# The pooled half of a mixer's input product taken from x times scale, its gate half after the shift is added, and a memory product in rounded parts

## The chip, the cores and the metric

One core of a Trainium2 chip runs the whole program. The metric is the device time of one execution in microseconds, as the median of several runs. Five engines work side by side, each through its own queue in order: TensorE (PE, with PEld for its weight loads), VectorE (DVE), ScalarE (ACT), GpSimd (POOL, unused here but for constants) and SyncE (SP, which issues every DMA).

## The reference, cut to what matters

Two blocks follow each other, all in fp32, for 512 tokens of 2048 channels. The change is in the first block and in one product of the second.

```
shift, scale, gate = split(silu(c) @ w_mod + b_mod, 3)       # w_mod: 2048 x 6144
h = rms_norm(x) * (1 + scale) + shift                        # 512 x 2048
u, g = split(h @ w_in, 2)                                    # w_in: 2048 x 4096 (w_pin)
pooled_i = centred_window_mean(u_i, w_i) - u_i               # 4 groups of 512 channels, w = 2, 4, 8, 16
y = (pooled_i @ w_grp_i) * pool_scale
x = x + gate * ((y * silu(g)) @ w_out)                       # w_pout
...                                                          # second block
mkv = rms_norm(mem) @ w_mem_kv                               # 256 x 2048 by 2048 x 1024 (w_kv)
```

`shift` and `scale` are one value per channel, the same for every token. So what `shift` adds to a column of u is the same for every token, and a mean over tokens less the token itself takes it out again (the mean divides by the number of tokens inside the sequence). The gate half g needs the whole h.

## The kernel before, in words

**Layout.** The activations of the first block lie with channels on the partitions: 16 chunks of 128 channels by 512 tokens. A large product goes in rounded parts: a number is split into a part that the rounded type holds (`whi`, `h_h`) and the exact rest (`wlo`, `h_l`), and three matmuls (hi by hi, hi by lo, lo by hi) make one (`mm3`, L254). `chan_tile` (L282) holds weights still and moves activations, `tok_tile` the other way round. Banks of PSUM are m0 to m3 and s0 to s3.

**The weight stream.** `Stream` (L34) goes through a plan of tiles in the order of their use. A tile of 512 KB is loaded by SP into one of three buffers (`raw`); `_piece` splits it in two halves, each a cast on ACT (L81) and a subtraction on DVE (L82), and the buffer is loaded anew when the second half has been split (L87 to L89). `take` keeps two halves split ahead; there are four buffers for split halves. `whole` hands a tile over unsplit. A tile with a key isn't split but added up on DVE by `gemv` (L423): DVE multiplies 512 columns of w_mod by a value of silu(c) per partition and adds them to an accumulator (L436). A second stream, `mod`, with up to nine buffers, does that for shift and scale.

**Work beside the main work.** Each part of the main work calls `step`, which gives credit to two lanes of generators (`aside` with a rate): lane 1 makes h, lane 0 does all else. `drain` runs a lane to its end at that place of the program. All engines take their instructions in the order in which this program writes them out.

**Order of the work.** First the memory product: 16 tiles of w_kv, taken whole, 64 matmuls in full fp32 (loop at L483, `mm` at L505) of `memt` (memory rows turned to channels, `mem_pair` L356, an ACT product with a gain out of PSUM). Beside it, rows of x are normed and turned (`x_prep` L391), and the first tiles of w_mod are added up. `modulation` (L455) then makes h two chunks at a time: 8 tiles, each with 256 columns of shift and 256 of scale; `col_sums` (L438) adds over partitions with 8 small matmuls per group, in PE's queue behind the last product of DVE; `make_h` (L443) gives x times scale plus shift on ACT, its cast `h_h`, and DVE makes `h_l` (L467). The input product begins beside that: 4 column tiles of u and 3 of g for each two chunks that are ready (L521 to L527); five more column tiles are begun over the first half of the channels (`begin`, L529) and kept in `early`, to be finished later. Then come the rest of g's and u's first groups, and the other groups in turn, u before g (`pool_loop` L623). `pooled` (L571) makes the window means on DVE in lane 0, `grp_tile` (L603) drains that lane and multiplies by w_grp, `y_out` (L609) takes the result times `pool_scale` times silu(g) and splits it into y_h and y_l. The output product (`tok_tile` with y, L671 on) takes tiles of w_mod for the gate in its stream too (`gate_part` L637).

Of the kernel before, what the change touches and what calls it, by code (L numbers as in the profile page):

```python
# [7 lines left out]
F32 = mybir.dt.float32  # L8
# [6 lines left out]
P = 128  # L15
# [10 lines left out]
# rows of the packed table of vectors  # L26
# [3 lines left out]
# column ranges of w_in_2  # L30
# [3 lines left out]
class Stream:  # L34
    """Weights in the order of their use: loaded ahead, split ahead into a rounded part and the exact rest."""
# [24 lines left out]
    def _piece(self):  # L60
        """One half of a tile of weights is split, or one tile of w_mod added up."""
# [59 lines left out]
def _build(es, tc, nc, x, vecs, bgate, fg, sinks, bforget, w_mod, w_pin, w_grp, w_pout, mem, w_in, w_kv,  # L121
# [7 lines left out]
    # ------------------------------------------------------------ plan of the weight stream  # L129
# [5 lines left out]
    # column tiles of the mixer's input product that begin with the first half of the channels, and how many  # L135
    # of them stand before each pair of chunks of the second half
    EARLY = [2048 + 384, 512, 640, 768, 896]
    AFTER = (1, 2, 2, 0)

# [3 lines left out]
    for kp in range(4):  # L143
        ent(w_pin, kp, [(0, 512, 0)])
        ent(w_pin, kp, [(2048, 384, 0)], n=384)
    ne = 0
    for kp in range(4, 8):
        for c0 in EARLY[ne : ne + AFTER[kp - 4]]:
            ent(w_pin, 0, [(c0, 128, 0)], n=128, kc=8)
        ne += AFTER[kp - 4]  # L150
        ent(w_pin, kp, [(0, 512, 0)])
    for kp in range(4, 8):
        ent(w_pin, kp, [(2048, 512, 0)])

    # products that take tiles of w_grp, by whether the product begins whole or half way
    GRP_AT, GRP_LATE = (3, 6), (4, 6)

    def plan_group(w, segs, n=512, grp=None, gate=None, k0=0):
        for kp in range(k0, 8):
# [3 lines left out]
            if grp is not None and kp in (GRP_AT if k0 == 0 else GRP_LATE):  # L163
                ent(w_grp, 0, [(0, 512, 0)], row0=512 * grp + 256 * (kp == 6))

    plan_group(w_pin, [(512, 512, 0)], grp=0, k0=4)
    plan_group(w_pin, [(2560, 512, 0)], grp=1)
    for g in (2, 3):
        plan_group(w_pin, [(512 * g, 512, 0)])
        plan_group(w_pin, [(2048 + 512 * g, 512, 0)], grp=g)  # L170
# [51 lines left out]
    # ------------------------------------------------------------ side work  # L222
# [12 lines left out]
    def step():  # L235
        """One part of the main work is out: some of the work beside it may follow."""
# [22 lines left out]
    def tile_steps(banks, k0, one, first, last, evac):  # L259
        """One tile of weights: half by half, the last tile of a sum bank by bank."""  # L260
# [21 lines left out]
    def chan_tile(banks, k0, ah, al, first, last, evac=None):  # L282
        """One tile of weights held still; the activations of its rows move."""
# [7 lines left out]
    def tok_tile(banks, k0, ah, al, first, last, n=512, evac=None):  # L291
        """One tile of weights moves; the activations of its rows are held still."""
# [7 lines left out]
    def rsqrt(pool, y, ss, inv, n):  # L300
        """y = 1 / sqrt(ss * inv + EPS), with a Newton step after the table's square root."""
# [1001 lines left out]
```

## Time and profile before

| | |
|---|---|
| device time, median of 3 runs | 2304.04 us (2301.97 to 2304.19) |
| span of the profiled execution | 2301.5 us; its own device time isn't listed apart |
| TensorE busy | 2269.5 us, 99% |
| VectorE busy | 1136.3 us, 49% |
| ScalarE busy | 802.8 us, 35% |
| DMA | 275.16 MB, mean 120 GB/s |

The span runs from the first to the last instruction of the core; the device time is a little longer. "Busy" of TensorE counts a matmul from its start to its modelled end, so that overlapping matmuls count once and a full PE says nothing of its clock; the granted clock stands in rows of their own, 1.00 for 2.4 GHz and 0.50 for 1.2 GHz. DVE's and ACT's shares are means over stages that differ.

### The profile page before, as it was taken

The page shows a single profiled execution, that of the slowest core. Times are in us where ns is not written, and L with a number is a line of the kernel's source. Part 1 is how long each engine was busy: PE and PEld are TensorE (multiplying, and loading weights), DVE is VectorE, ACT ScalarE, POOL GpSimd, SP SyncE. Part 2 cuts the span into 40 slices and gives each one's busy share as a digit, 9 for nine tenths or more (in the row PEclk, how much of TensorE's full clock was granted, in tenths as well). Part 3 has the DMA queues.
Part 4 walks back from the last instruction along what each step waited for, and adds up shares of the span by engine and source line. Part 5 has one row for each costly group of instructions (what it writes and reads, how often), then busy time and mean ns, then how long its engine had stood idle before and what let it go on. Part 6 is the DMA issues. An engine that isn't in the chain of part 4 may idle for free.

```text
span 2301.5 us, 27608 instructions
## 1 busy us (share of the span) xinstructions
PE 2269.5 (99%) x10615; PEld 1862.3 (81%) x10615; DVE 1136.3 (49%) x2009; ACT 802.8 (35%) x1545; POOL 0.2 (0%) x4
## 2 busy tenths in 40 slices
PE   8889999999999999999999999999999999999999
PEld 4578888887889988888888888788888888888887
DVE  3776544356665444566644444455225335226333
ACT  4333332333334443434353434442222222223221
POOL 0000000000000000000000000000000000000000
PEclk9989999999999999999999999999999999999999
DMA  8994333336774332222222222233333333333443
GB/s 290 327 312 125 99 97 98 100 111 220 223 223 138 103 83 74 74 65 75 73 73 64 74 61 77 59 98 101 92 101 93 100 98 95 101 92 97 151 136 110
DMA packets 188203, 275.16 MB, mean 120 GB/s; under 512 B 12082, under 2 KB 98600, under 8 KB 187816
## 3 DMA queue, kind: packets, MB, share of 16 engines
q1 hardware_dynamic: 188072, 273.41, 39.2%
q8 instruction: 83, 1.36, 0.2%
q14 instruction: 48, 0.39, 0.1%
HBM read 264.98 MB, written 8.39 MB: 119 GB/s over the span
## 4 chain that ended last, share of the span: by engine, by line
PE 92%; DMA 4%; DVE 2%; ACT 1%; SPq 1%; issue 1%; DVEq 0%; ACTq 0%
PE m L252 60%; PE s L252 29%; DMA raw<-w_mod 2%; PE s L1020 1%; DMA raw<-w_pin 1%; DMA raw<-w_pout 1%; DVE acc L436 1%; PE s L826 1%; DVE wlo L82 0%; DMA nat<-mem 0%; PE s L1059 0%; PE s L406 0%; DMA xg_d<-xg 0%; PE colb L252 0%; PE s L703 0%
## 5 line engine op out<-in xcount | busy, mean ns | idle before, releaser
L82 DVE TENSOR_TENSOR wlo<-raw,whi 128x512 fp32r<-128x512 f32 (+2 forms) x738 | 493.2, 677 | 733.2 <-ACT whi L81 722.2
L81 ACT CAST whi<-raw 128x512 fp32r<-128x512 f32 (+2 forms) x738 | 443.1, 609 | 862.7 <-PE m L252 412.9
L252 PE MATMUL m<-whi,h_h 128*128 128x512 f32 (+2 forms) x960 | 374.4, 390 | 1.3 <-ACT whi L81 1.3
L252 PE MATMUL m<-wlo,h_h 128*128 128x512 f32 (+2 forms) x960 | 361.9, 377 | 0.8 <-DVE wlo L82 0.7
L252 PE MATMUL m<-whi,h_l 128*128 128x512 f32 (+2 forms) x960 | 362.0, 377 | 0.0
L252 PE MATMUL m<-h_h,whi 128*128 128x512 f32 x736 | 290.9, 395 | 4.3 <-ACT whi L81 4.0
L252 PE MATMUL m<-h_l,whi 128*128 128x512 f32 x736 | 288.3, 392 | 0.4 <-DVE h_l L467 0.4
L252 PE MATMUL m<-h_h,wlo 128*128 128x512 f32 x736 | 288.1, 391 | 0.0
L252 PE MATMUL s<-h_h,whi 128*128 128x512 f32 x544 | 214.2, 394 | 0.0
L252 PE MATMUL s<-h_l,whi 128*128 128x512 f32 x544 | 213.4, 392 | 0.0
L252 PE MATMUL s<-h_h,wlo 128*128 128x512 f32 x544 | 213.3, 392 | 0.0
L252 PEld LDWEIGHTS m<-whi,h_l 128*128 128x128 f32 x960 | 180.4, 188 | 31.7
L252 PEld LDWEIGHTS m<-whi,h_h 128*128 128x128 f32 x960 | 180.6, 188 | 30.7 <-ACT whi L81 1.6
L252 PEld LDWEIGHTS m<-wlo,h_h 128*128 128x128 f32 x960 | 180.8, 188 | 27.6 <-DVE wlo L82 1.6
L252 PEld LDWEIGHTS m<-h_h,whi 128*128 128x128 f32 x736 | 139.2, 189 | 33.1 <-ACT whi L81 4.1
L252 PEld LDWEIGHTS m<-h_h,wlo 128*128 128x128 f32 x736 | 138.9, 189 | 29.4 <-DVE wlo L82 0.3
L252 PEld LDWEIGHTS m<-h_l,whi 128*128 128x128 f32 x736 | 139.2, 189 | 29.0 <-DVE h_l L467 1.1
L252 PEld LDWEIGHTS s<-h_h,whi 128*128 128x128 f32 x544 | 103.5, 190 | 21.6
L252 PEld LDWEIGHTS s<-h_l,whi 128*128 128x128 f32 x544 | 103.4, 190 | 21.6
L252 PEld LDWEIGHTS s<-h_h,wlo 128*128 128x128 f32 x544 | 103.2, 190 | 21.7
L252 PE MATMUL m<-whi,y_h 128*128 128x512 f32 x256 | 102.6, 401 | 1.6 <-DVE t L733 1.5
L252 PE MATMUL m<-whi,y_l 128*128 128x512 f32 x256 | 99.9, 390 | 0.0
(233 smaller groups left out, 2846.6 us busy)
## 6 DMA issues: line engine op xcount, KB each, us to landing
raw<-w_in SPq DMA_DIRECT2D x96, 512.0 KB, 3.8
raw<-w_mod SPq DMA_DIRECT2D x128, 256.0 KB, 5.8
raw<-w_pin SPq DMA_DIRECT2D x61, 512.0 KB, 3.7
raw<-w_in SPq DMA_DIRECT2D x96, 256.0 KB, 2.9
raw<-w_mod SPq DMA_DIRECT2D x32, 512.0 KB, 4.1
raw<-w_pout SPq DMA_DIRECT2D x32, 512.0 KB, 4.0
raw<-w_out SPq DMA_DIRECT2D x32, 512.0 KB, 3.7
raw<-w_in SPq DMA_DIRECT2D x32, 384.0 KB, 3.4
```

What stands on the lines that cost most here:

```text
L81: self.nc.scalar.copy(h3, v)
L82: self.nc.vector.tensor_tensor(out=l3, in0=v, in1=h3.bitcast(F32), op=ALU.subtract)
L252: PE.matmul(ps, lhsT=lhsT, rhs=rhs, start=start, stop=stop)
L436: V.scalar_tensor_tensor(out=acc, in0=v[:, e, :], scalar=w, in1=acc, op0=mult, op1=add)
L826: PE.transpose(b[:, i * P : (i + 1) * P], s, idf)
L1020: PE.transpose(b[:, i * P : (i + 1) * P], pt[:, i * P : (i + 1) * P], idf)
```

## The change

Four things change.

- **The memory product** goes through `tile_steps`: w_kv is split like other weights, `mem_pair` makes the rounded memory rows on ACT and their rest on DVE (out of PSUM), and three matmuls stand where one in full fp32 stood.
- **xs in place of h.** `mod` reads scale alone, 32 tiles of 512 columns; four chunks of x times scale are made at a time (`make_xs`). Four column tiles of u's first group and three of its second go over all 16 chunks in one pass; the last tile of the second group follows by itself. `early` goes.
- **The order of the mixer**: u of all four groups first, then g of all four. Pooling and grouped tiles stand beside u's third and fourth group and the first of g (the table `GRP`); the grouped result times `pool_scale` waits in `yr`, and y is made when a bank of g is evacuated (`evac_g`). `pooled` handles two chunks per instruction.
- **The shift**: its half of w_mod enters the weight stream in 32 tiles of 1024 columns, 2 per pair of chunks, summed on DVE into `sacc`. Ahead of the last pair of u's fourth group 16 small matmuls add it up over partitions, and `add_shift` adds it to the 16 chunks and splits them anew, before and beside g's first group.

```diff
-    for kp in range(4):
+    for kp in range(8):
         ent(w_pin, kp, [(0, 512, 0)])
-        ent(w_pin, kp, [(2048, 384, 0)], n=384)
...
+        ent(w_pin, kp, [(512, 384, 0)], n=384)
+    shifts = [(k, c) for k in range(NK) for c in range(2)]
+    def plan_shift(n):
+        for k, c in shifts[:n]:
+            ent(w_mod, 0, [(1024 * c, 1024, 0)], n=1024, kc=1, row0=k * P, key=("s", c, k))
+        del shifts[:n]
+    for r in range(2):
+        ent(w_pin, 0, [(896, 128, 0)], n=128, kc=8, row0=1024 * r)
+        plan_shift(2)
+    GRP = {2: {2: (0, 0), 4: (0, 1), 7: (1, 0)}, 3: {2: (1, 1), 4: (2, 0), 6: (2, 1)}, 4: {3: (3, 0), 6: (3, 1)}}
+    def plan_group(w, segs, n=512, grp={}, gate=None, shift=0):
+        for kp in range(8):
             if gate is not None:
                 ent(w_mod, kp, [(4096 + 512 * gate, 512, 0)], key=("g", gate, kp))
             ent(w, kp, segs, n=n)
+            plan_shift(shift)
+            if kp in grp:
+                ent(w_grp, 0, [(0, 512, 0)], row0=512 * grp[kp][0] + 256 * grp[kp][1])
+    for g in range(2, 8):
+        plan_group(w_pin, [(512 * g, 512, 0)], grp=GRP.get(g, {}), shift=2)
...
-    mod_plan = [("G", w_mod, j2 * 256, 2, 512, [(256 * kp, 256, 0), (2048 + 256 * kp, 256, 256)], ("h", kp, j2))
-                for kp in range(8) for j2 in range(8)]
+    mod_plan = [("G", w_mod, j2 * 256, 2, 512, [(2048 + 512 * q, 512, 0)], ("h", q, j2)) for q in range(4) for j2 in range(8)]
...
-            S.activation(m[:, c, :], b[:, c * MEM : (c + 1) * MEM], AF.Copy, scale=cols[:, R_MG + k : R_MG + k + 1])
+            S.activation(mh[:, c, :], b[:, c * MEM : (c + 1) * MEM], AF.Copy, scale=g)
+            V.scalar_tensor_tensor(out=ml[:, c, :], in0=b[:, c * MEM : (c + 1) * MEM], scalar=g, in1=r32(mh[:, c, :]), op0=mult, op1=sub)
...
+    def make_xs(k):
+        scl = a0.tile([P, 1], F32, tag="scl", name="scl", bufs=4)
+        V.tensor_tensor(out=scl, in0=colb[:, k : k + 1], in1=bsc1[:, k : k + 1], op=add)
+        S.activation(xnT[k], xnT[k], AF.Copy, scale=scl)
+        S.copy(h_h[k], xnT[k])
...
+        for q in range(5):
             for j in range(8):
+                if q < 4:
                     mod._piece()
                     yield
+                k = 4 * q - 4 + j
+                if q and j < 4:
+                    make_xs(k)
                     yield
+                if q and 1 <= j < 5:
+                    V.tensor_tensor(out=h_l[k - 1], in0=xnT[k - 1], in1=r32(h_h[k - 1]), op=sub)
                     made[0] += 1
                     yield
...
+    def mem_one(ps, b, k, wh, wl, start, stop):
+        c = slice(b * P, (b + 1) * P)
+        mm3(ps, memt[k][0][:, c], memt[k][1][:, c], wh, wl, start, stop)
...
-            w = st.whole()
-            for i in range(2):
-                for j in range(2):
-                    mm(mb[c][i], memt[2 * kp + j][:, i * P : (i + 1) * P], w[:, j, :], start=kp + j == 0, stop=kp == 7 and j == 1)
+            tile_steps(mb[c], 2 * kp, mem_one, kp == 0, kp == 7, ev_mem(c))
...
+    for kp in range(8):
+        while made[0] <= 2 * kp + 1:
             advance(1)
         if kp == 0:
+            pace(0.7)
+        chan_tile(ub, 2 * kp, h_h, h_l, kp == 0, kp == 7)
+        chan_tile(u1, 2 * kp, h_h, h_l, kp == 0, kp == 7)
...
+    def evac_g(g):
+        yh = yhp.tile([P, 4, T], F32R, tag=f"yh{g}", name=f"y_h{g}")
+        def ev(b, ps):
+            k = 4 * g + b
+            y_h[k] = yh[:, b, :]
+            sg = a1.tile([P, T], F32, tag="sg", name="sg", bufs=2)
+            S.activation(sg, ps, AF.Silu)
+            V.tensor_tensor(out=sg, in0=yr[k], in1=sg, op=mult)
+            S.copy(y_h[k], sg)
+            y_l[k] = yp.tile([P, T], F32R, tag=f"yl{k}", name=f"y_l{k}")
+            V.tensor_tensor(out=y_l[k], in0=sg, in1=r32(y_h[k]), op=sub)
+        return ev
...
+    def pool_loop(evac, grp={}, before=None):
         banks = [bank(t) for t in M4]
         for kp in range(8):
+            if before is not None:
+                before(kp)
             chan_tile(banks, 2 * kp, h_h, h_l, kp == 0, kp == 7, evac=evac)
+            if kp in grp:
+                i, cp = grp[kp]
+                grp_tile(i, cp, pool[0])
+                if cp:
+                    aside(grp_out(i), 0.5)
+                if (i, cp) not in ((2, 1), (3, 1)):
+                    pool[0] = new_pool(i + cp, 1 - cp)
...
+    def add_shift():
+        for k in range(NK + 1):
+            if k < NK:
+                S.activation(xnT[k], xnT[k], AF.Identity, bias=shf[:, k : k + 1])
+                S.copy(h_h[k], xnT[k])
+            if k:
+                V.tensor_tensor(out=h_l[k - 1], in0=xnT[k - 1], in1=r32(h_h[k - 1]), op=sub)
+                shifted[0] += 1
+            yield
...
+    def begin_shift(kp):
+        if kp < 7:
+            return
+        drain()
+        sb = bank("s3", "shb")
+        for k in range(NK):
+            mm(sb[:, k : k + 1], sacc[k // 8][:, (k % 8) * P : (k % 8 + 1) * P], ones[:, 0:1], start=True, stop=True)
+        V.tensor_tensor(out=shf, in0=sb[:, 0:NK], in1=cols[:, R_BMOD : R_BMOD + NK], op=add)
+        aside(add_shift(), 0.5, 1)
+    pool_loop(evac_u(2), grp=GRP[2])
+    def after_shift(kp):
+        while shifted[0] <= 2 * kp + 1:
+            advance(1)
+    pool_loop(evac_u(3), grp=GRP[3], before=begin_shift)
+    pool[0] = new_pool(3, 0)
+    pool_loop(evac_g(0), grp=GRP[4], before=after_shift)
     for g in range(1, 4):
-        if g > 1:
-            pool_loop(evac_u)
-        pool_loop(evac_g, grp=g)
-        aside(y_out(g), 0.25)
+        pool_loop(evac_g(g))
```

## Rows read from the trace of the kernel before

**Rows 1.** The page: the span, each engine's busy time (share of the span, instructions), and in 40 equal slices of the span the tenths in which TensorE was busy and the clock granted to it.
```profile
span 2301.5 us, 27608 instructions
...
PE 2269.5 (99%) x10615; PEld 1862.3 (81%) x10615; DVE 1136.3 (49%) x2009; ACT 802.8 (35%) x1545; POOL 0.2 (0%) x4
...
PE   8889999999999999999999999999999999999999
...
PEclk9989999999999999999999999999999999999999
```

**Rows 2.** Busy time by stage (the view by stretches): stretch in us, its length, then busy us and instructions of PE, PEld, DVE, ACT and POOL, the mean granted clock, the DMA share and GB/s. The stages are the memory product, the part in which h is made beside the first columns of the mixer's input product, the rest of the mixer, and all that follows.
```profile
13.00:80.00 67.00, 67.00 (x216) 33.86 (x216) 30.82 (x80) 28.94 (x74) 0.00 (x0) 1.00 0.92 310
80.00:202.00 122.00, 107.63 (x473) 88.55 (x472) 100.41 (x174) 41.90 (x70) 0.00 (x0) 0.87 0.89 276
202.00:516.00 314.00, 314.00 (x1387) 260.01 (x1386) 155.57 (x261) 100.71 (x169) 0.00 (x0) 1.00 0.33 100
516.00:2301.50 1785.50, 1777.78 (x8534) 1477.39 (x8532) 848.74 (x1488) 626.94 (x1226) 0.00 (x0) 1.00 0.35 104
```

**Rows 3.** TensorE's instructions in order of time, alike ones merged: start in us, us, engine, line, operation, tiles, count, and in brackets the idle time before and what ended it.
```profile
13.20 9.55 PE L252 MATMUL m<-raw,memt 128*128 128x512 f32 x16
...
59.27 20.77 PE L252 MATMUL m<-raw,memt 128*128 128x512 f32 x48
79.87 1.84 PE L252 MATMUL colb<-ones,acc 128*128 128x1 f32 x16
85.72 0.79 PE L252 MATMUL m<-h_h,whi 128*128 128x512 f32 x1 [4.01 <-ACT whi L81]
...
88.87 0.63 PE L252 MATMUL m<-h_l,whi 128*128 128x512 f32 x1
89.30 0.63 PE L252 MATMUL m<-h_h,wlo 128*128 128x512 f32 x1
```

**Rows 4.** Groups of TensorE's instructions from 0 to 240 us, shapes apart: tiles, shapes, count, busy us, mean ns of one, idle before it.
```profile
L252 PE MATMUL m<-raw,memt 128*128 128x512 f32 x128 | 60.6, 614 | 0.0
...
L252 PE MATMUL colb<-ones,acc 128*128 128x1 f32 x128 | 19.7, 278 | 9.6 <-DVE acc L436 9.5
```

**Rows 5.** What TensorE waited for between 80 and 200 us: tile and line, who was waited for, us in total, times, longest.
```profile
PE colb L252 <- DVE acc L436: 9.5, 7, 3.3
PE m L252 <- ACT whi L81: 4.0, 1, 4.0
```

**Rows 6.** Stretches of 4 us in which the clock fell and came back (columns as in rows 2).
```profile
108.00:112.00 4.00, 3.07 (x18) 2.89 (x19) 4.00 (x8) 0.00 (x0) 0.00 (x0) 0.80 1.08 361
112.00:116.00 4.00, 4.00 (x11) 3.13 (x10) 3.12 (x7) 3.18 (x5) 0.00 (x0) 0.50 1.10 350
116.00:120.00 4.00, 4.00 (x16) 3.20 (x16) 4.00 (x7) 0.51 (x2) 0.00 (x0) 0.84 1.09 354
...
160.00:164.00 4.00, 3.92 (x17) 3.79 (x17) 3.01 (x8) 0.44 (x1) 0.00 (x0) 0.50 0.90 273
164.00:168.00 4.00, 4.00 (x11) 3.03 (x11) 1.05 (x2) 3.47 (x6) 0.00 (x0) 0.50 1.08 334
168.00:172.00 4.00, 4.00 (x18) 3.29 (x17) 4.00 (x7) 0.00 (x0) 0.00 (x0) 0.94 0.90 266
```

**Rows 7.** Groups of ScalarE's instructions from 0 to 530 us (columns as in rows 4).
```profile
L81 ACT CAST whi<-raw 128x512 fp32r<-128x512 f32 x146 | 88.9, 620 | 146.1 <-PE m L252 97.6 <-PE s L252 37.2 <-issue 9.7
...
L450 ACT ACTIVATE xq<-xq,shf,scl 128x512 f32<-128x512 f32 x16 | 13.0, 813 | 45.4 <-DVE scl L448 45.4
...
L451 ACT CAST h_h<-xq 128x512 fp32r<-128x512 f32 x16 | 9.9, 620 | 0.5
L565 ACT ACTIVATE sg<-m 128x512 f32<-128x512 f32 x12 | 7.2, 598 | 9.7 <-PE m L252 9.7
```

**Rows 8.** The same of VectorE, and at the end one line of its instructions in order of time.
```profile
L82 DVE TENSOR_TENSOR wlo<-raw,whi 128x512 fp32r<-128x512 f32 x145 | 99.0, 690 | 147.8 <-ACT whi L81 139.7 <-PE s L252 8.0
L436 DVE SCALAR_TENSOR_TENSOR acc<-raw,csil,acc 128x512 f32<-128x512 f32 x112 | 77.0, 749 | 0.0
...
L592 DVE TENSOR_TENSOR pl<-praw,ph 128x512 fp32r<-128x512 f32 x16 | 11.1, 693 | 11.1 <-ACT ph L591 11.1
L590 DVE SCALAR_TENSOR_TENSOR praw<-tr,up 128x512 f32<-128x512 f32 x16 | 11.1, 693 | 0.6
...
L467 DVE TENSOR_TENSOR h_l<-xq,h_h 128x512 fp32r<-128x512 f32 x16 | 10.9, 691 | 6.7 <-ACT h_h L451 6.7
...
L434 DVE TENSOR_SCALAR acc<-raw,csil 128x512 f32<-128x512 f32 x16 | 7.0, 484 | 0.0
...
L448 DVE TENSOR_TENSOR scl<-colb,bsc 128x2 f32<-128x2 f32 x8 | 1.2, 155 | 0.0
...
59.64 4.06 DVE L436 SCALAR_TENSOR_TENSOR acc<-raw,csil,acc 128x512 f32<-128x512 f32 x6
```

**Rows 9.** DMA issues by line, each with its count, KB and the median us from issue to landing: the two of w_pin and w_grp from 202 to 516 us, that of w_mod from 500 to 560.
```profile
raw<-w_pin SPq DMA_DIRECT2D x46, 512.0 KB, 3.7
raw<-w_grp SPq DMA_DIRECT2D x8, 512.0 KB, 3.7
...
raw<-w_mod SPq DMA_DIRECT2D x9, 512.0 KB, 4.3
```

**Rows 10.** The instructions that read the tile y_h, over the whole span: count, least, median and largest ns, first and last start in us.
```profile
L252 PE MATMUL m<-whi,y_h x256: 387/389/799, 515.8 to 701.0; 128*128 128x512 f32 x128
```

More of the change, by code (lines that the diff above doesn't have):

```diff
@@ L318, in _build @@
     mkv = kvpool.tile([P, 2, 1024], F32, name="mkv")
-    ep = ExitStack()
-    earlyp = ep.enter_context(tc.tile_pool(name="early", bufs=1, side="right"))
-    early = {}
+    yhs = ExitStack()
+    yhp = yhs.enter_context(tc.tile_pool(name="yhp", bufs=1))
+    xq = [yhp.tile([P, 4, T], F32, tag=f"yh{q}", name=f"xq{q}") for q in range(4)]
+    xnT = [xq[k // 4][:, k % 4, :] for k in range(NK)]
     p0 = ExitStack()
@@ L375, in _build @@
     mem_pair(1)
-    xq = [a0.tile([P, 4, T], F32, name=f"xq{q}") for q in range(4)]
-    xnT = [xq[k // 4][:, k % 4, :] for k in range(NK)]
     ssq = a0.tile([P, 6, 4], F32, name="ssq")
@@ new lines, in pooled @@
+        src, s0, span = up, 8 - w // 2, 1
+        while span < w:
+            n = T + w - 2 * span
+            t = a1.tile([P, 2, 528], F32, tag=f"tr{span % 3}", name="tr", bufs=1)
+            V.tensor_tensor(out=t[:, :, :n], in0=src[:, :, s0 : s0 + n], in1=src[:, :, s0 + span : s0 + span + n], op=add)
+            src, s0 = t, 0
+            span *= 2
+            yield
+        hw = w // 2
+        e0 = edg[:, i, 0, :hw].unsqueeze(1).to_broadcast([P, 2, hw])
+        V.tensor_tensor(out=src[:, :, :hw], in0=src[:, :, :hw], in1=e0, op=mult)
@@ new lines, in pooled @@
+        if hw > 1:
+            e1 = edg[:, i, 1, : hw - 1].unsqueeze(1).to_broadcast([P, 2, hw - 1])
+            V.tensor_tensor(out=src[:, :, T - hw + 1 : T], in0=src[:, :, T - hw + 1 : T], in1=e1, op=mult)
+        praw = a1.tile([P, 2, T], F32, tag="praw", name="praw")
+        V.scalar_tensor_tensor(out=praw, in0=src[:, :, :T], scalar=1.0 / w, in1=up[:, :, 8:520], op0=mult, op1=sub)
+        yield
+        S.copy(ph, praw)
+        yield
+        V.tensor_tensor(out=pl, in0=praw, in1=r32(ph), op=sub)
@@ L595, in _build @@
+        yield
     grp_banks = {}
     def new_pool(i, cp):
-        ph = [a1.tile([P, T], F32R, tag=f"ph{c}", name="ph") for c in range(2)]
-        pl = [a1.tile([P, T], F32R, tag=f"pl{c}", name="pl") for c in range(2)]
-        aside(pooled(i, cp, ph, pl), 0.32)
-        return ph, pl
+        ph = a1.tile([P, 2, T], F32R, tag="ph", name="ph")
+        pl = a1.tile([P, 2, T], F32R, tag="pl", name="pl")
+        aside(pooled(i, cp, ph, pl), 0.3)
+        return [ph[:, c, :] for c in range(2)], [pl[:, c, :] for c in range(2)]
@@ L607, in grp_tile @@
         chan_tile(grp_banks[i], 0, pool[0], pool[1], cp == 0, cp == 1)
-    def y_out(i):
-        yrs = {}
-        for ct in range(5):
-            if ct < 4:
-                yrs[ct] = a1.tile([P, T], F32, tag="yr", name="yr", bufs=2)
-                k = 4 * i + ct
-                V.scalar_tensor_tensor(out=yrs[ct], in0=grp_banks[i][ct], scalar=cols[:, R_PS + k : R_PS + k + 1], in1=sg[:, ct, :],
-                                       op0=mult, op1=mult)
-                S.copy(y_h[k], yrs[ct])
-            if 0 < ct < 5:
-                k = 4 * i + ct - 1
-                V.tensor_tensor(out=y_l[k], in0=yrs[ct - 1], in1=r32(y_h[k]), op=sub)
-            yield
@@ L623, in pool_loop, with grp_out, ev @@
-    def pool_loop(evac, grp=None):
+    def grp_out(i):
+        for ct in range(4):
+            k = 4 * i + ct
+            S.activation(yr[k], grp_banks[i][ct], AF.Copy, scale=cols[:, R_PS + k : R_PS + k + 1])
+            yield
+    def evac_g(g):
+        yh = yhp.tile([P, 4, T], F32R, tag=f"yh{g}", name=f"y_h{g}")
+        def ev(b, ps):
+            k = 4 * g + b
[6 more added lines that the diff above has]
+            V.tensor_tensor(out=y_l[k], in0=sg, in1=r32(y_h[k]), op=sub)
+        return ev
@@ new lines, in _build, with shift_part @@
+    sacc = [a1.tile([P, 1024], F32, name=f"sacc{c}") for c in range(2)]
+    def shift_part(c, k, v):
+        w, v = csil[:, k : k + 1], v[:, 0, :]
+        if k == 0:
+            V.tensor_scalar(out=sacc[c], in0=v, scalar1=w, scalar2=None, op0=mult)
+        else:
+            V.scalar_tensor_tensor(out=sacc[c], in0=v, scalar=w, in1=sacc[c], op0=mult, op1=add)
+    more["s"] = shift_part
+    shf = a1.tile([P, NK], F32, name="shf")
+    shifted = [0]
+    def add_shift():
[6 more added lines that the diff above has]
+                shifted[0] += 1
+            yield
@@ L759, in _build @@
     ys.close()
+    yhs.close()
     us = ExitStack()
```

149 lines of the change are left out of this document (27 added, 122 removed).

## The prediction

> **What bounds the kernel now.** I first read the page's totals and slices: PE is busy for 2269.5 of 2301.5 us, and only the first slices show less than full tenths or a clock below full [rows 1]. So only two things can move the time: PE work that goes away, and time near the start in which PE waits or runs at its lower clock. The busy time by stage says where that is [rows 2]. From 13 to 80 us, the memory product, PE has no gap and a full clock. (Its first 16 records, at 0.60 us each, show a slow start, [rows 3].) From 80 to 202, the part in which h is made piece by piece, it is busy 107.6 of 122 us at a mean granted clock of 0.87. From 202 to 516 it is full, and so nearly to the end.
>
> One matmul of rounded parts costs 314.0 / 1387 = 0.226 us of PE time at the full clock [rows 2]; its listed 0.39 us overlaps with the next. At the lower level two starts lie 0.43 apart, at 88.87 and 89.30 [rows 3]. A memory matmul in full fp32 shows as two records, and 48 records take 20.77 us: 0.433 a record, 0.865 a matmul [rows 3]. Sixteen records of column sums take 1.84 us, 0.23 a sum [rows 3].
>
> What is lost between 80 and 202: of 473 records 112 are column sums (the 128 of [rows 4] less the first 16), 112 x 0.115 = 12.9 us; the other 361 x 0.226 = 81.6. That makes 94.5 of 122 us: **27.5 us are lost**. PE waited 9.5 us for the accumulators under the column sums and 4.0 for a split weight [rows 5], and behind such waits the clock fell to 1.2 GHz (0.50 in the rows) for some 6 to 10 us at a time [rows 6]. DVE was busy 100.4 us of it and DMA moved 276 GB/s [rows 2]: 33.5 MB of w_mod had to be read and summed up before h was whole.
>
> **The change, part by part.**
>
> *Memory product.* 64 fp32 matmuls (55.4 us) become 192 of rounded parts (43.5): **11.9 us of PE work go** if the clock stays full. But the parts must be split: 32 casts on ACT at 0.62 (19.8 us, on 28.9 busy: 48.7) [rows 2, 7] and 32 subtractions on DVE at 0.69 (22.1), with 16 subtractions of 256 columns out of PSUM, which before doesn't have; between 0.15 us (a tiny operation's price, [rows 8]) and 0.75 (512 columns with a scalar, [rows 8]) I take 0.4, since half the columns stand nearer the middle: 6.4 us. DVE comes to 30.8 + 22.1 + 6.4 = 59.3 us [rows 2, 8], while PE's work, transposes included, is 67 - 11.9 = 55 us. So DVE, not PE, fills the stage, in order behind norms and transposes, and PE starts some 2 us later since its first weights must be split. I take 63 us from 13 on, DVE at 94%: the end at 76 in place of 80, so **8 us of the 11.9 are given back** (0 to 12; beyond 12 is a rival).
>
> *Column sums.* Eight groups of 8 sums become four of 8 and sixteen single ones later: 64 to 48, **3.7 us go**.
>
> *xs in place of h.* Half of w_mod, 16.8 MB, stands ahead of the pooled half. Seven banks now take all 16 chunks in one pass: 336 matmuls, 76 us, so each quarter of w_mod (4 chunks, two pairs) has 19 us of PE cover. At the pace of 0.7 a step, a quarter's 16 parts take 23 steps, 1.63 pairs: 15.5 us and 1.84 of sums, 17.4. In these DVE does 16 products at 0.68 (6 in 4.06 us, [rows 8]), 4 low parts at 0.69 and the weights' low parts, 1.63 pairs of 2.4 us: 17.5. DMA brings 4.2 MB and 1.5 of weights, 328 GB/s, under the 350 to 361 of the rows in which it ran without a pause [rows 6]. Level, not over, and the last 3.6 pairs have no more of it. **Of the 27.5 us, I leave 2 of waits and one fall of the clock, 3.5** (8 us at half rate, less overlap): 5.5 (0 to 16, a wait and a fall at each of three quarters).
> Ahead of the first product stay the scale's addition, an ACT product with one scalar (0.81, [rows 7]), a cast (0.62) and a subtraction (0.69). The weights are split already, which was the 4.0 us of before. I take **1.9 us of idle and 2.5 of slow clock** (2 to 8).
>
> *Shift beside it.* 32 tiles of 1024 columns enter the weight stream, 2 per pair, on the same three buffers and the same SP queue. DVE takes 32 x 1.36 = 43 us for them, beside 16 pairs' splits (22), six grouped tiles' (8) and the pooling of three groups (some 28, from 0.69 per 512 columns, [rows 8]): 101 of the 120 us of two loops and six grouped tiles. It fits on average. The buffers are tighter: three tiles per pair means each buffer turns once in 24 x 0.226 = 5.4 us. A tile lands in 3.7 us alone and 4.3 beside w_mod [rows 9], and a weight tile then needs two casts and a subtraction, 2.0, and the next issue 0.1: 6.4. A grouped tile, 5.4 us of PE for one buffer, follows every second or third pair and gives the slack back (10 tiles in 21.7 us leave a buffer 6.5). I take **3 us lost** (0 to 13, every one of 14 pairs late by 0.95).
> The Trainium skill, "DMA: Bandwidth & Descriptors", section "Anatomy of one DMA", gives 2.0 us and bytes over 436 GB/s per transfer, fitted for transfers issued from GpSimd. For 512 KB that is an estimate of 3.2 us; the turn would be 5.3 and this term 0. The rows with 3.7 to 4.3 on the queue used here speak against it.
>
> *Pooling.* Two chunks go in one instruction at the same cost per column. The low part now stands three dependent operations of 1024 columns deep. At two grouped tiles (the third group's) the side work has 16 steps for what needs 20 to 28, so it is drained with PE behind it: praw, ph and pl at 1.3 + 1.2 + 1.3, less two halves of lead (2.7 us): **2.5 us** for both (0 to 6).
>
> *Adding the shift.* Its 16 sums wait for the last of four ACT copies out of a bank, with the group's last pair behind them in PE's queue: some **1.2 us**. Then ACT has 16 x 1.24 us beside casts and copies, 29 us for five pairs and a grouped tile (33 us): **1.5 us** (0 to 5).
>
> *Gates last.* Each of four evacuations is Silu, product, cast, subtraction per bank, and the next bank's Silu stands in ACT's queue behind the cast, which waits for DVE: 0.6 + 0.7 + 0.6 and the handovers come to 2 us against 1.36 us of PE per bank, so the fourth bank is freed about 2.5 us after PE's last matmul, and the next loop needs it after 2.0. With a table load: **2.5 us** over all (0 to 5). Before, products waited for nobody here [rows 2].
>
> Nothing after the mixer is touched: the first product of y stands at 515.8 [rows 10], and what follows keeps its length. SP issues 64 transfers of w_mod where it issued 128 (512 KB each, not 256), and one more of w_pin.
>
> **The sum.** 11.9 + 3.7 + 27.5 = 43.1 gone; 8 + 5.5 + 4.4 + 3 + 2.5 + 2.7 + 2.5 = 28.6 back: 14.5 us. The profiled span 2301.5 gives 2287.0. Its own device time isn't listed apart; the median of the runs, 2304.04, stands 2.5 us above the span, and I keep that: **2289.5 us**.
>
> **The rivals.**
> 1. *The memory product runs at the lower clock* (slower). Fed by DVE it waits often, where fp32 never did. At 0.43 a matmul its work is 82.6 us, 39 more, and the 8 us of waits vanish in it: -14.5 + 31 = +16.5, **2320**. It decides once some 110 of the 192 run so: (14.5 + 8) / 0.204. For it: at 85% busy the clock was at half for a quarter of the time [rows 2, 6]. Against: a PE at half rate is slower than DVE, becomes full, and a full PE was given its clock back each time [rows 6]. Chance 0.10. The Trainium skill, "TensorE: Matmul & The Clock Gate", section "HAM oscillation", tells of a kernel throttled anew at every tile because each waited for data; by that rule this rival would come. The trace agrees as far as long waits go and shows none so short.
> 2. *Everything is covered.* Memory ends at 72, quarters cost nothing, the small terms halve: 43.1 - 4 - 3 - 6.5 = 30, **2274**. For it: even between 80 and 202 DVE had 18% to spare [rows 2]. Chance 0.17.
> 3. *Three buffers don't feed 1.6 MB per pair.* The shift term is 13: gain 4.5, **2299.5**. Chance 0.12.
> 4. *The rounded product isn't shorter*, because DVE or the transfers (22 MB by the last w_kv tile) end it at 80 as before: gain 10.5, **2293.5**. Chance 0.13.
> The forecast keeps 0.48, its own range 2282 to 2297.
>
> **How the numbers follow.** What a measurement here can tell from no change is 0.2%, 4.6 us. Faster takes the forecast, rivals 2 and 4 and a third of 3: 0.82. Same is the rest of 3, 0.08; slower is rival 1, 0.10. The range reaches down into rival 2 and up past rival 3, and leaves out rival 1 and the far end of 2: 2271 to 2303.
>
> **What the changed profile would show.** Memory's last matmul near 76; first product of xs near 80; the seven banks done near 169; PE's first product of y near 501 in place of 515.8; granted clock above 0.95 from 80 to 200. A clock of 0.5 over the memory stage, or PE waiting for casts between 180 and 300 at every pair, would show rivals 1 or 3. Wrong it would also be if work after the mixer moved.

## The result, and the profile after

The changed kernel takes **2325.8 us** (median of 4 runs, 2324.93 to 2326.93) beside 2304.1 for the kernel before on the same chip: ratio 1.0093, 95% interval 1.0079 to 1.0108. It is 21.7 us slower where 14.5 us less were forecast: 2325.8 against 2289.5, a miss of 36.3 us.

First the page: PE's busy time hardly changed, but its first slices did (compare [rows 1]).

```profile
span 2323.5 us, 27655 instructions
...
PE 2269.0 (98%) x10647; PEld 1873.0 (81%) x10647; DVE 1154.5 (50%) x1982; ACT 845.8 (36%) x1621; POOL 0.2 (0%) x4
...
PE   6899989999999999999999999999999999999999
...
PEclk9899999999999999999999999999999999999999
```

The stages, cut at the changed kernel's own ends (columns as in [rows 2]): the memory product up to the first column sum; the part that makes xs; the pooled half with the shift beside it; g's first group; the other gates; all that follows.

```profile
13.00:84.50 71.50, 61.00 (x279) 45.45 (x278) 54.12 (x123) 46.50 (x109) 0.00 (x0) 1.00 0.84 287
84.50:165.00 80.50, 68.14 (x282) 55.97 (x282) 55.13 (x104) 31.97 (x54) 0.00 (x0) 0.85 0.53 170
165.00:345.00 180.00, 169.96 (x728) 137.45 (x727) 107.88 (x136) 57.84 (x97) 0.00 (x0) 0.96 0.58 183
345.00:400.00 55.00, 55.00 (x242) 45.16 (x241) 37.31 (x53) 33.84 (x55) 0.00 (x0) 1.00 0.33 96
400.00:534.80 134.80, 132.05 (x579) 108.05 (x578) 49.96 (x75) 45.06 (x77) 0.00 (x0) 1.00 0.33 98
534.80:2323.50 1788.70, 1779.83 (x8535) 1478.61 (x8533) 848.18 (x1487) 626.47 (x1226) 0.00 (x0) 1.00 0.35 104
```

The first product of y (the tile's row, as [rows 10]) and, over the first 600 us, what PE waited for (columns as in [rows 5]):

```profile
L247 PE MATMUL m<-whi,y_h x256: 387/389/799, 534.8 to 723.7; 128*128 128x512 f32 x128
```

```profile
PE colb L247 <- DVE acc L433: 9.2, 5, 4.5
...
PE s L247 <- ACT ph L559: 6.1, 2, 5.1
PE m L247 <- DVE wlo L82: 4.0, 10, 1.2
PE m L247 <- ACT whi L81: 3.5, 3, 2.2
PE m L247 <- ACT sg L593: 3.2, 5, 1.5
PE s L247 <- DVE pl L561: 3.1, 3, 1.9
PE m L247 <- ACT h_h L445: 3.1, 1, 3.1
```

The first product of y stands 19.0 us later than before. What follows takes 1788.7 us instead of 1785.7; that part does the same work in every kernel of this document, and its length in their traces lies between 1785.5 and 1790.6 us, so these 3 us don't stand out as an effect of the change. I price each stage at the full clock as the prediction did, 0.2264 us a matmul and 0.115 a record of the column sums; what a stage takes beyond that is lost. From 84.5 to 165 the 282 records hold 64 of column sums: 218 x 0.2264 + 7.4 = 56.7 of 80.5 us, **23.8 lost**. From 165 to 345, 32 of 728 belong to the shift's sums: 161.3 of 180, **18.7 lost**. From 345 to 400 nothing, from 400 on 134.8 - 579 x 0.2264 = 3.7. The memory product ends at 84.5 instead of 79.9.

The views that follow show how the loss from 84.5 to 165 comes about. PE in order of time (columns as in [rows 3]), lines with a wait, and one at the lower clock:

```profile
89.56 0.80 PE L247 MATMUL m<-h_h,whi 128*128 128x512 f32 x1 [3.06 <-ACT h_h L445]
...
104.94 3.81 PE L247 MATMUL colb<-ones,acc 128*128 128x1 f32 x16 [4.50 <-DVE acc L433]
...
110.04 0.63 PE L247 MATMUL m<-h_h,whi 128*128 128x512 f32 x1
...
128.20 0.38 PE L247 MATMUL colb<-ones,acc 128*128 128x1 f32 x2 [1.37 <-DVE acc L433]
...
150.74 0.38 PE L247 MATMUL colb<-ones,acc 128*128 128x1 f32 x2 [2.79 <-DVE acc L433]
```

What DVE, then ACT, waited for from 88 to 155 us:

```profile
DVE wlo L82 <- ACT whi L81: 13.3, 9, 2.0
DVE scl L443 <- PE colb L247: 5.6, 3, 3.2
```

```profile
ACT xq L444 <- DVE scl L443: 44.5, 11, 10.6
```

And one round of it in order of time, DVE first, then ACT:

```profile
93.95 1.41 DVE L433 SCALAR_TENSOR_TENSOR acc<-raw,csil,acc 128x512 f32<-128x512 f32 x2
95.28 0.15 DVE L443 TENSOR_TENSOR scl<-colb,bsc 128x1 f32<-128x1 f32 x1
97.29 0.56 DVE L82 TENSOR_TENSOR wlo<-raw,whi 128x384 fp32r<-128x384 f32 x1 [1.86 <-ACT whi L81]
```

```profile
95.46 0.72 ACT L444 ACTIVATE xq<-xq,scl 128x512 f32<-128x512 f32 x1 [2.02 <-DVE scl L443]
...
96.74 1.55 ACT L81 CAST whi<-raw 128x384 fp32r<-128x384 f32 x3
```

PE stands still for an accumulator at the second to fourth quarter, and behind the wait of 4.50 us the 16 records of column sums take 3.81 us instead of the 1.84 of [rows 3]. DVE is not full over the stage (55.1 of 80.5 us). In the round shown, ACT waits 2.02 us at an xs for a scale, which stands on DVE behind two products of w_mod; ACT's cast of a weight stands behind that xs, and DVE then waits 1.86 us for the cast. Each engine, in order, waits for the other. Such rounds make up DVE's 13.3 us. Of ACT's 44.5 us, 31.9 are of another kind: four waits in which a whole quarter's column sums are still to come.

### The profile page after: what moved, and what is told of

Read it like the earlier page. It is cut to its first block, busy times and chain, and to the rows that moved or that the text cites. A ratio compares the mean times of both kernels' runs of the same rounds, so it can differ in the third digit from the quotient of the medians.

```text
span 2323.5 us, 27655 instructions
## 1 busy us (share of the span) xinstructions
PE 2269.0 (98%) x10647; PEld 1873.0 (81%) x10647; DVE 1154.5 (50%) x1982; ACT 845.8 (36%) x1621; POOL 0.2 (0%) x4
## 4 chain that ended last, share of the span: by engine, by line
PE 88%; DVE 4%; ACT 3%; DMA 2%; issue 1%; SPq 0%; ACTq 0%; DVEq 0%
PE m L247 57%; PE s L247 29%; PE s L1038 1%; DVE acc L433 1%; DVE wlo L82 1%; DMA raw<-w_pin 1%; ACT whi L81 1%; PE s L844 1%; DMA raw<-w_pout 1%; DMA raw<-w_grp 0%; ACT junk L384 0%; DVE sg L594 0%; PE colb L247 0%; DVE tr L546 0%; PE s L1077 0%
## 5 line engine op out<-in xcount | busy, mean ns | idle before, releaser
L82 DVE TENSOR_TENSOR wlo<-raw,whi 128x512 fp32r<-128x512 f32 (+3 forms) x772 | 513.6, 675 | 759.2 <-ACT whi L81 753.2
L81 ACT CAST whi<-raw 128x512 fp32r<-128x512 f32 (+3 forms) x772 | 460.8, 608 | 925.6 <-PE m L247 423.4
L247 PE MATMUL m<-h_h,whi 128*128 128x512 f32 x768 | 304.9, 397 | 5.8 <-ACT h_h L445 3.1
L247 PE MATMUL m<-h_l,whi 128*128 128x512 f32 x768 | 301.7, 393 | 0.0
L247 PE MATMUL m<-h_h,wlo 128*128 128x512 f32 x768 | 301.5, 393 | 0.0
L247 PE MATMUL s<-h_h,whi 128*128 128x512 f32 x512 | 200.3, 391 | 0.0
L247 PE MATMUL s<-h_l,whi 128*128 128x512 f32 x512 | 200.1, 391 | 0.0
L247 PE MATMUL s<-h_h,wlo 128*128 128x512 f32 x512 | 199.9, 390 | 0.0
L247 PEld LDWEIGHTS s<-h_h,whi 128*128 128x128 f32 x512 | 96.6, 189 | 20.1
L247 PE MATMUL m<-wlo,y_h 128*128 128x512 f32 x256 | 100.4, 392 | 0.3 <-DVE wlo L82 0.3
```

Of the source, the lines that this page charges most:

```text
L81: self.nc.scalar.copy(h3, v)
L82: self.nc.vector.tensor_tensor(out=l3, in0=v, in1=h3.bitcast(F32), op=ALU.subtract)
L247: PE.matmul(ps, lhsT=lhsT, rhs=rhs, start=start, stop=stop)
```

## The experiments

Times are medians, ratios are to the kernel before run beside them (2304.1 to 2304.6 us each time), and "less" or "slower" without a name is against the changed kernel's 2325.8. Line numbers in a kernel's rows are its own.

**The part that makes xs.** Column sums later in PE's queue:

```diff
+            late = 2 if q > 1 else 0
...
+                if q and j == late:
+                    col_sums(q - 1)
+                k = 4 * q - 4 + j - late
...
-            if q < 4:
-                col_sums(q)
```

> The changed kernel with the column sums of the second to fourth quarter put two tiles of w_mod later in TensorE's queue; the same work. Theory A (VectorE is only a few us late at the three sums, since a quarter's last products come bunched, and each wait of 1.4 to 4.5 us also costs a fall of the clock): the waits under the sums between 100 and 155 us go below 1 us each, the granted clock stays near 1 and the time falls by 10 to 16 us (2310 to 2316). Rival B (VectorE has too much work per quarter): the wait moves to the first product that needs the next chunks, and the time falls by 0 to 3 us.

2321.95 us (2321.48 to 2323.88), ratio 1.0078 [1.0063, 1.0093]: 3.9 less, between the two. PE's waits for accumulators fall from 9.2 to 4.8, one of 3.8 stays. Where PE stands in its queue is a small part.

The scales of four chunks added at once, before the next w_mod products; ACT's xs issued ahead of the next w_mod tile; side work at 0.5 a step instead of 0.7:

```diff
+    def make_scl(q):
+        scl4[q] = a0.tile([P, 4], F32, tag="scl", name="scl", bufs=2)
+        V.tensor_tensor(out=scl4[q], in0=colb[:, 4 * q : 4 * q + 4], in1=bsc1[:, 4 * q : 4 * q + 4], op=add)
...
+                if q and j == late:
+                    col_sums(q - 1)
+                    make_scl(q - 1)
+                if q and 0 <= j - late < 4:
+                    make_xs(k)
                 if q < 4:
                     mod._piece()
...
-            pace(0.7)
+            pace(0.5)
```

> The changed kernel with the four scales of a quarter added in one VectorE operation behind the sums, and each chunk's product with its scale issued on ScalarE ahead of VectorE's next w_mod tile, not behind it; the pace is 0.5 in place of 0.7 since there are fewer parts, so that a quarter takes the same stretch of the program. Theory A (VectorE and ScalarE wait for each other: a scale stands behind 1.35 us of w_mod, a cast behind that scale's two operations, a low part behind the cast, 13.3 us of VectorE's waits in 65 us): those waits fall below 6 us, the waits under the sums below 3 us in all, and the time falls by 10 to 15 us (2311 to 2316). Rival B (too much work per quarter): 0 to 3 us.

2313.28 us (2310.55 to 2315.21), 1.0034 [1.0022, 1.0047]: **12.5 less**, theory A. The stage, what DVE waited for in it from 88 to 155 us, and what PE still waited for an accumulator:

```profile
84.50:165.00 80.50, 77.13 (x356) 64.02 (x355) 59.83 (x102) 35.33 (x61) 0.00 (x0) 0.96 0.60 197
```

```profile
DVE scl L444 <- PE colb L247: 6.0, 3, 3.0
DVE wlo L82 <- ACT whi L81: 5.0, 5, 1.4
```

```profile
PE colb L247 <- DVE acc L433: 0.3, 1, 0.3
```

In the same 80.5 us PE issues 356 records instead of 282, at 0.96 of the clock instead of 0.85, and its waits under the sums fall from 9.2 us to 0.3. Priced as above, 292 matmuls and 64 records of sums are 73.5 of 80.5 us: 7.0 lost, where it was 23.8. DVE does more work in the stage, not less, so most of the loss was the order in the queues and not the volume. The edit has three parts, and these runs don't tell how much each gives. (The pace goes with the other two: a quarter now has 12 parts of side work in place of 16, so at 0.5 it takes 24 steps of the main work, and 23 before.)

More split halves ahead (six buffers, four ahead) while u's first group runs:

```diff
+        st.ahead = 4 if kp < 6 else 2
+        if kp == 7:
+            st.hlp = hlp
```

> The changed kernel with six buffers for split weight halves and four split ahead, in place of four and two, while the seven banks of u are summed (the pool of the first stage has room for it). Theory A (VectorE idles there since the next cast waits for a buffer that TensorE still reads, so it cannot work ahead of the sums): VectorE's waits for the cast between 90 and 155 us shrink, and the time falls by 6 to 12 us (2314 to 2320). Rival B (order and volume of the w_mod products decide, not the buffers): within 2 us.

2327.83 us (2325.88 to 2329.66), 1.0102 [1.0087, 1.0117]: no gain. DVE's wait for ACT's casts stays 13.5 us; more buffers for split halves don't mend this order of the queues.

**The shift's stream.** The shift left out (its half of w_mod is neither read nor added, so the gates are computed without it):

```diff
-        for k, c in shifts[:n]:
+        for k, c in []:
...
-        aside(add_shift(), 0.5, 1)
```

> The changed kernel without the shift: its half of w_mod isn't loaded or summed, and nothing is added to the chunks, so the gate half lacks it. Theory A (the shift beside the pooled half costs what is lost from 165 to 345 us, 18.7 us, and its sums 3.7): the time falls by 18 to 22 us (2304 to 2308). Rival B (pooling two chunks at once, drained in front of PE, costs most of it by itself): it falls by 4 to 10 us, and PE still waits for pooled parts at 308 us.

2304.91 us (2302.76 to 2308.02), 0.9998 [0.9989, 1.0007]: 20.9 less, theory A. The shift and all that hangs on it cost that; the prediction's terms for it were 3 in the stream, 2.7 in adding it, and its 16 sums.

A fourth buffer for loaded tiles, from the pooled half until the last group of g begins, so for all of the shift's tiles in it:

```diff
+            self.turn = (self.turn + 1) % 4
+            pl = self.raw2 if self.turn == 0 else self.raw
...
+    st.raw2 = p1.enter_context(tc.tile_pool(name="raw2", bufs=1))
+    st.bufs = 4
```

> The changed kernel with a fourth buffer for loaded tiles while the shift's tiles are in the weight stream. Theory A (three tiles per pair turn three buffers in 4.0 us of landing and 2.0 of splitting, longer than the 5.4 us of a pair, so splits come late and with them pooling): PE's waits between 200 and 330 us (9.2 us) go below 3 us and the time falls by 8 to 14 us against the changed kernel (2312 to 2318). Rival B (the pooling's own order and rate hold PE): 0 to 2 us.

2313.01 us (2310.39 to 2317.43), 1.0032 [1.0019, 1.0046]: **12.8 less**, theory A. How one more buffer does that, the changed kernel shows: ACT from 283 us on, and SP's issues.

```profile
287.17 1.14 ACT L81 CAST whi<-raw 128x512 fp32r<-128x512 f32 x2 [1.75 <-DMA raw<-w_pin]
293.23 0.62 ACT L81 CAST whi<-raw 128x512 fp32r<-128x512 f32 x1 [4.91 <-DMA raw<-w_pin]
...
300.04 1.14 ACT L81 CAST whi<-raw 128x512 fp32r<-128x512 f32 x2 [3.35 <-DMA raw<-w_grp]
```

```profile
283.17 0.38 SPq L51 DMA_DIRECT2D raw<-w_pin  x1
284.37 2.22 SPq L51 DMA_DIRECT2D raw<-w_mod  x2
289.15 0.38 SPq L51 DMA_DIRECT2D raw<-w_pin  x1
```

The next weight tile is issued 6.0 us after the last, when its buffer comes free, and its cast begins 4.1 us later still. From 165 to 345 us ACT's casts wait like this in all:

```profile
ACT whi L81 <- DMA raw<-w_pin: 36.0, 11, 5.6
```

With the fourth buffer this is 17.3 us, and in the kernel without the shift none. The low part behind the cast holds up DVE, and the pooling stands behind it there, in order. DVE's next lines, and PE's at the grouped tile:

```profile
300.69 0.69 DVE L82 TENSOR_TENSOR wlo<-raw,whi 128x512 fp32r<-128x512 f32 x1 [2.05 <-ACT whi L81]
301.30 1.23 DVE L546 TENSOR_TENSOR tr<-up 128x1036 f32<-128x1036 f32 x1
...
305.84 1.23 DVE L557 SCALAR_TENSOR_TENSOR praw<-tr,up 128x1024 f32<-128x1024 f32 x1
```

```profile
308.20 0.80 PE L247 MATMUL s<-ph,whi 128*128 128x512 f32 x1 [5.11 <-ACT ph L559]
...
310.48 0.63 PE L247 MATMUL s<-ph,whi 128*128 128x512 f32 x1
```

So PE never waits for a cast at a pair; it stops at the grouped tiles, where the late pooling is drained, and goes on at the lower clock. With the fourth buffer the stage and PE's waits for pooled parts (6.1 and 3.1 us in the changed kernel) read

```profile
165.00:345.00 180.00, 177.19 (x785) 145.51 (x784) 117.90 (x149) 70.92 (x117) 0.00 (x0) 0.99 0.59 189
```

```profile
PE s L252 <- ACT ph L564: 1.3, 1, 1.3
...
PE s L252 <- DVE pl L566: 0.8, 1, 0.8
```

The other explanation, that pooling is merely credited too slowly:

```diff
-        aside(pooled(i, cp, ph, pl), 0.3)
+        aside(pooled(i, cp, ph, pl), 0.6)
...
-                    aside(grp_out(i), 0.5)
+                    aside(grp_out(i), 1.0)
```

> The changed kernel with the side work of pooling issued at twice its rate (0.6 and 1.0 a step in place of 0.3 and 0.5), so that it is out before its grouped tile. Theory A (TensorE waits for pooled parts that the side work issued too late, 8.8 us in waits at 237, 263 and 308 us, and twice loses its clock): these waits go below 2 us in all and the time falls by 8 to 12 us (2314 to 2318). Rival B (the parts are late because the weight stream with three buffers is late in these loops): the time falls by 0 to 3 us.

2330.49 us (2329.05 to 2332.9), 1.0115 [1.01, 1.013]: 4.7 slower. Pooling issued earlier stands ahead of the low parts on DVE, and PE now waits for splits too (3.9 us from 84 to 345, none in the changed kernel), with 3.9 still waited for ph.

**The memory product.** Back in full fp32 (`mem_pair` makes one fp32 tile again):

```diff
-            tile_steps(mb[c], 2 * kp, mem_one, kp == 0, kp == 7, ev_mem(c))
+            w = st.whole()
+            for i in range(2):
+                for j in range(2):
+                    mm(mb[c][i], memt[2 * kp + j][:, i * P : (i + 1) * P], w[:, j, :], start=kp + j == 0, stop=kp == 7 and j == 1)
```

> The changed kernel with one part undone: the memory product again in 64 full-fp32 matmuls of unsplit weights, the rest as changed. Theory A (the rounded product is fed too slowly by VectorE and ScalarE and ends at 84.5 us where fp32 ended at 80): the product ends near 80, the first product of xs starts near 85 in place of 89.6, and the time falls by 4 to 6 us against the changed kernel (2320 to 2322). Rival B (the stage is set by its transfers, or what is won is waited for again at the next sums): within 2 us of the changed kernel. My recorded forecast, by which the rounded parts win 4 us, would make it 4 us slower than the changed kernel.

2320.87 us (2316.39 to 2323.46), 1.0076 [1.0058, 1.0094]: 4.9 less, theory A. The first column sum comes at 79.2 us, nearly as before (79.9); the first product of xs follows only at 86.7, behind a wait of 5.7 us for a split weight. And the rounded product alone in the kernel before (the edit reversed):

> The kernel before with one part of the change alone: the memory product in rounded parts. Theory A (fed by VectorE and ScalarE it ends some 4.6 us later than fp32): 3 to 6 us slower than the kernel before (2307 to 2310). Rival B (in the kernel before the stage that follows is bound by transfers, which go on meanwhile, so that the delay is made good): within 2 us of it. By my recorded forecast it would be 4 us faster.

2311.72 us (2309.97 to 2314.15), 1.0031 [1.002, 1.0042]: 7.6 slower than before, more than the 3 to 6 expected, first column sum at 84.4, PE waiting 4.5 us for the first h. Two comparisons from either side agree on the sign, not on the size. Why the stage is long: what DVE, then ACT, waited for from 13 to 84.5 us in the changed kernel.

```profile
DVE wlo L82 <- ACT whi L81: 8.5, 6, 2.5
DVE meml L364 <- ACT memh L363: 4.9, 8, 1.1
DVE rx L301 <- ACT rs_t L300: 2.2, 5, 1.2
DVE ssx L393 <- ACT junk L384: 1.8, 3, 0.7
```

```profile
ACT memh L363 <- DVE meml L364: 11.6, 7, 3.0
```

DVE's 54.1 us of work and 17.4 of waits, all for ACT, are the 71.5 us of the stage. The 11.6 us looked like two memory chunks sharing a tile, so each got its own:

```diff
-        mh = a0.tile([P, 2, MEM], F32R, tag="memh", name="memh", bufs=4)
+            mh = a0.tile([P, MEM], F32R, tag=f"memh{c}", name="memh", bufs=4)
```

> The changed kernel with each chunk of the memory rows in a tile of its own, and nothing else. Theory A1: the product ends 3 us or more before 84.5 and the time falls by 3 to 5 us (2321 to 2323). Rival A2 (VectorE's work sets the end): 0 to 2 us.

2324.54 us (2322.12 to 2326.2), 1.0084 [1.007, 1.0098], 1.3 less: my first theory fell. The sums still begin at 84.7 us, and ACT still waits 10.6 us for meml. Then more split halves ahead, over the memory product alone:

```diff
+    hl2 = p0.enter_context(tc.tile_pool(name="hl2", bufs=6))
+    st.hlp, st.ahead = hl2, 4
```

> The changed kernel with six buffers for split halves and four halves split ahead over the memory product alone (two ahead, four buffers, as before, from there on). Why does the rounded product end at 84.5 us instead of 76? Theory L (lookahead): PE waits because a half is asked for two halves after it was begun and a transposed memory chunk stands between; with four ahead TensorE's waits for whi and wlo there (3.5 and 4.0 us) fall below 3, the first column sum moves from 84.5 to 77 to 81 and the time falls by 3 to 8 us: 2318 to 2323. Rival V (volume): VectorE's low parts, norms, transposed chunks and column products fill the stage whatever the order: the column sum stays within 2 us of 84.5 and the time within 2 us of 2325.8.

2319.65 us (2317.58 to 2324.01), 1.0071 [1.0054, 1.0088]: 6.2 less, in the range of theory L, but not by its way. The first column sum:

```profile
85.47 0.38 PE L247 MATMUL colb<-ones,acc 128*128 128x1 f32 x2 [2.01 <-DVE acc L433]
```

PE is done with the product at 83.5, 1.0 us earlier, and then waits for DVE's accumulator: DVE's queue ends the stage. The first product of y comes 3.8 us earlier (531.0). These are won in the next part, where the wait of 4.50 us is down to 0.2 and 301 records in place of 282 stand in the 80.5 us; how the edit does that, no run shows. With the other two repairs in, the same edit gave nothing (below), so I don't count it as a cause of its own.

**Together.** The fourth buffer and the scales at once (the two diffs above; "the run before" in the expectation is the kernel with three repairs, which follows here):

> As the run before, but with the memory product in rounded parts as in the change. Theory A: 2325.8 less 12.5 and 12.8, 2299 to 2302. Rival B: 2305 to 2310. Its difference to the kernel with three repairs prices the rounded product once more: 4 to 6 us if what it loses isn't made good later.

2298.07 us (2296.99 to 2301.07), 0.9971 [0.9959, 0.9983]; a little faster than theory A's 2299 to 2302: the two gains of 12.5 and 12.8 add up (27.7 together). With the memory product in fp32 as well:

> The changed kernel with three repairs at once: the memory product back in fp32, ScalarE's product with the scale ahead of the w_mod tile, and the fourth buffer beside the shift. Theory A (three separate losses, alone worth 4.9, 12.5 and 12.8 us, that add up): 2294 to 2298, some 6 to 10 us faster than the kernel before. Rival B (each repair wins the same time, since what is early in one stage waits in the next): 2305 to 2310.

**2293.88 us** (2292.63 to 2296.08), 0.9952 [0.9939, 0.9964]: faster than both kernels, and 4.2 us faster than with the rounded product, the third price for it beside 4.9 and 7.6. Its stages (columns as above), and its first product of y:

```profile
84.50:165.00 80.50, 78.23 (x350) 64.46 (x351) 56.56 (x96) 34.28 (x60) 0.00 (x0) 0.94 0.59 190
165.00:345.00 180.00, 177.21 (x779) 143.88 (x779) 126.49 (x160) 79.51 (x130) 0.00 (x0) 0.99 0.58 188
```

```profile
L252 PE MATMUL m<-whi,y_h x256: 387/389/799, 503.3 to 690.9; 128*128 128x512 f32 x128
```

The rounded product with the two repairs and a tile per memory chunk, and with the two repairs and more halves ahead:

> The kernel with two repairs, and each chunk of the memory rows in a tile of its own, so that ScalarE's second product of a pair doesn't wait for VectorE's first subtraction (12.2 us of such waits in the changed kernel). Theory A1 (that handover is what keeps the rounded product from ending early): the product ends 3 us or more before 84.5 and the time falls by 3 to 5 us against the kernel with two repairs. Rival A2 (VectorE's 54 us of work in the stage, near full from 60 us on, set its end): 0 to 2 us.

> The same, with the scales of four chunks added at once and ScalarE's xs ahead of the next w_mod tile, and with the fourth loaded-tile buffer beside the shift: the kernel with these two repairs took 2298.1 us, the one with the memory product back in fp32 as well 2293.9. Theory L: 3 to 8 us less, 2290 to 2295, first product of y at 501 to 506 (509.0 without). Rival V: 2296 to 2300, first product of y within 2 us of 509.

2300.72 us (2298.93 to 2301.04), 0.9982 [0.9972, 0.9991], and 2300.43 (2296.78 to 2304.92), 0.9982 [0.9972, 0.9993]: neither is better than 2298.07 without. With four halves ahead the sums again wait 2.0 us for DVE (first one at 85.3). Rival V: the order of the splits isn't it. Of V's two halves, DVE's own work and its waits for ACT, these runs don't tell which would have to go.

## Why the prediction was wrong

Its description of the kernel before stood in the main: time was lost between 80 and 202 us, and 2293.9 us shows that some 10 us of it could be had. What failed are three terms of the sum, all by one mistake: **an engine was judged by the sum of its work against the stage ("level, not over", "it fits on average"), and an in-order queue that waits (for another engine's queue, or for the turn of a buffer) was counted at nothing or nearly so.**

- *Memory product*, "8 us of the 11.9 are given back". It gave back 16.5: the end at 84.5, not 76, **8.5 missed**. DVE was taken at 59 us and 94% busy; it had 54 us of work and was busy 76%, with 17.4 us of waits for ACT. The price of a subtraction out of PSUM, taken at 0.4 us, measured 0.48, 1.3 us more for all 16, so the price was not it. That these waits, and not DVE's own work, are the loss isn't shown: no edit here took them away. Rival 4 (the end at 80) was the right doubt and too mild.
- *Quarters*, "5.5", and *ahead of the first product*, "4.4". 23.8 us were lost against 9.9: **13.9 missed**. Ahead of the first product it was as sized: 3.1 of idle and eight matmuls at 0.43 (1.6) against 1.9 and 2.5. The three later quarters waited 9.2, with a stretch at the lower clock behind each. Over the stage nothing was full: DMA 0.53, DVE 68%. The step named products, low parts and bytes, but never asked what a scale stands behind on DVE, nor what a cast stands behind on ACT. The edit that reorders these, and sets the pace to match, gave 12.5 us.
- *Shift stream*, "3", pooling "2.5" and adding the shift "2.7". Measured 18.7 from 165 to 345, and nothing while the shift is added up to 400, against 8.2 in all: **10.5 missed**. Here the working had it: a buffer turns in 6.4 us (measured 6.0 between issues) and PE needs it in 5.4; I then trusted the slack of the grouped tiles. Rival 3, at 0.12, was the case, with its 13 us (12.8 from the fourth buffer). Only its sign was another: not PE waiting for casts at every pair, but ACT's casts waiting for loaded tiles (36.0 us for w_pin's), DVE behind them, and PE stopping at the grouped tiles for the pooling queued there. (DVE's waits for casts by themselves are no sign of it: 48.2 us from 165 to 345, but 79.7 in the kernel without the shift, where they cost PE next to nothing.)
- *Gates last*, "2.5": 3.7 lost, 3.2 of it waits for ACT. Right in kind, 1.2 more.

Together 34.1, against the 33.5 by which the first product of y missed its place (534.8, not 515.8 - 14.5 = 501.3); the 3 us after it are within what the traces differ by there.

Three readings in the prediction were off as well, and moved it little. [rows 3] show the first 16 records of column sums from 79.87 on, so nearly all of them are among the 473 from 80 to 202, out of which the prediction took them: with 128 records at 0.115 us and 345 at 0.2264, 29.2 us were lost there, not 27.5. PE was 88% busy there, not 85%. Pooling's 3.8 less 2.7, for two tiles, is 2.2 and not 2.5.

Rival 1, the way I gave to "slower", did not happen: the granted clock of the memory stage was 1.00, though PE was 85% busy there and waited 7.2 us for splits, no more than 2.2 at once. (That longest wait stands ahead of its first matmul; the first matmuls stand 0.43 us apart until 21.3 us, as slow a start as that of [rows 3], which the mean of 1.00 doesn't show.) The Trainium skill, "TensorE: Matmul & The Clock Gate", section "HAM oscillation", tells of a kernel throttled anew at every tile because each waited for data. This trace shows no fall behind the stage's later waits, of 0.2 to 1.65 us, and falls behind those for accumulators, of 1.4, 2.8 and 4.5 us. The waits in that page's kernel are long ones for transfers, so "by that rule this rival would come" read more into it than it says.

Without the memory product's 3.9 us of gain the forecast's own sum is 2293.4; the kernel with the two repairs and that product in fp32 took 2293.9. So the remaining terms are about right as a total, once the queues and the buffers are mended; that the two numbers agree to half a microsecond is luck.

## What to carry to other kernels

Where two in-order engines feed each other, write down for each instruction on the way to the bound what stands ahead of it in its own queue and whom that waits for; load against length of the stage doesn't show it. If a loop has a buffer whose turn (landing, split, issue) is longer than the work it covers, take the loss as real, and look for it at the next place where side work is drained. Small dependent steps (here the scales) go ahead of long independent ones in the queue; pooling, which is long itself, made it slower when it was put ahead.

## What the hardware showed that was not expected

- In the changed kernel a wait of 1.37 us (and one of 0.28 behind it) for accumulators was followed by a stretch at the lower clock, matmul starts 0.43 us apart from 130.4 to 134 us. In the memory product of the same trace a wait of 1.65 us, ahead of a transposition at 57.8 us, was not (the next starts stand 0.25 to 0.32 us apart), nor were nine of 0.2 to 1.2 us for low parts. The length of a wait alone doesn't tell here whether the clock falls.
- Beside the shift's tiles a weight tile took hardly longer to land: 3.8 us from its issue in the median of w_pin's tiles from 165 to 345 us, where 3.7 is the median of [rows 9]; the w_mod tiles took 4.6. In a loop of three buffers that and the split are the whole 6.0 us of a turn, and with four buffers the time falls although w_pin's tiles then take 4.4 us to land.
